# A fused decoder layer on one core: attention steps in another order, its rotation on VectorE, rotary tables in five parts, half of the first round's additions on VectorE

## The chip, the cores and the metric

The kernel runs on one core of one Trainium2 chip. The metric is device time in microseconds (us) from the start to the end of one execution; a few executions of the same kernel give the median and the interval that are shown below. Of one execution there is a profile: the time of every instruction on every engine. TensorE is called PE in it, VectorE DVE, ScalarE ACT, GpSimd POOL and SyncE SP.

## The reference, cut to what matters

One layer over 512 positions of 1024 features, in float32: a gated feed-forward block (FFN), a mixing block of three head groups side by side, and a second FFN. Each reads an RMS-normed copy of x and adds its result to x.

```python
x = x + 0.5 * swiglu(rms_norm(x, g_ffn1), w_gate1, w_up1, w_down1)
h = rms_norm(x, g_mix)
q, k, v, u, mq = split(h @ w_in)
q = rope_partial(rms_norm(q, g_q), positions)      # 16 of a head's 64 rows turn
k = rope_partial(rms_norm(k, g_k), positions)
y_attn = sliding_window_attention(q, k, v, sinks)  # 8 heads, 2 k/v heads, window 128
y_conv = silu(layer_norm(depthwise_conv(a * sigmoid(gate), 31 taps)))
y_mem  = memory_cross_attention(rms_norm(mq), mk, mv)   # 4 heads, 256 memory rows
x = x + concat(y_attn, y_conv, y_mem) @ w_out
x = x + 0.5 * swiglu(rms_norm(x, g_ffn2), w_gate2, w_up2, w_down2)
```

## The kernel before, in words

Activations stand transposed: features on the 128 partitions, the 512 positions along a row. A float32 product is made of three products of rounded halves: `whi` and `wlo` are the two halves of a weight tile, `xh`/`xl`, `yh`/`yl`, `hh`/`hl`, `bh`/`bl` those of activations. A 512-column product is the line trio L347, L348, L349 (`mm3`); a 256-column one is L444, L445, L446. Each weight tile comes by DMA into `wraw`; ACT rounds it (`whi`, L167) and DVE subtracts (`wlo`, L168). Four buffers each hold these halves, used in turn, so a cast waits until PE has read the tile of four turns before. A scheduler places the instructions of each engine in one fixed order; an instruction that waits holds up all that stands behind it on its engine.

**FFN.** 22 tiles f of hidden features. From the fifth on, `fast(f)` makes gate and up by seven 256-column block products instead of eight. Partial sums leave PSUM by ACT copies into `kept` (L455, L459, L461), DVE adds them (L464, L475, L479), ACT takes silu (L465) and rounds the hidden tile (`hh`, L402), DVE subtracts (`hl`, L403). `down(r, g)` multiplies finished tiles with the down weights, in rounds r of some tiles each, two outputs d per weight tile g in round 0. A result is added to x by DVE (L506), or in round 0 by an ACT copy (L502) and a POOL transfer that adds in memory (L503). `rotary` makes the sine and cosine tables for the later rotation: a range reduction on DVE (L701 to L713), then Sin, Abs, Sin on ACT (L714, L715, L717). It is one hook behind tile 9 of the first FFN.

**Mixing.** The steps stand in the list `ORDER`, written by hand: each name is a function that records its instructions for all engines. `pX` is the projection of tile X (48 instructions: L347 to L349), `sumX` the sums of squares of two tiles over a head, on PE with a 2-column operand (L814, from ACT's squares L805), `facX` their inverse roots, a chain of small operations on DVE (L826 to L834, L332 to L337), `ropeX` the rotation (L839 to L842), `scoresX` the score products on PE (L865; 64 rows, 128 or 256 columns), `softX` the masked maximum on DVE (L883, then `neg` L892, L895) and the exponentials on ACT (L901), `weightsX` the division (L914 to L923), `turnX` transposes of the weights on PE (L936) with copies to `pt` (L939), `valuesX` the products with v (L950) with `yh`/`yl` (L966, L967), `outD_KS` the output product of tile D over the parts KS of y, `c` one more tap of the convolution on DVE (L793, two instructions), `ln_...` its layer norm. S0 to S3 are the four pairs of query heads, M0 and M1 the memory heads, K the keys. The rotation is a shuffle on DVE (L839), a product with the sine table on POOL (L840), a product with the cosine table on DVE (L841), and an addition (L842). Behind the list come the output products over parts 4 and 5 (weights `wb`), then over 6 and 7 (`wc`), whose `yh`/`yl` are the convolution's and come from `ln_swish` (transposes L1026, a multiplication L1084, silu L1085, then L966, L967).

## Time and profile before

| | |
|---|---|
| median of 3 runs | 875.81 us (874.29 to 877.52) |
| the profiled execution's own time | 874.01 us |
| its span, first to last instruction | 872.2 us |
| PE busy | 863.5 us (99%) |
| DVE busy | 697.7 us (80%) |
| ACT busy | 449.2 us (51%) |
| POOL busy | 46.3 us (5%) |
| mean granted clock of TensorE | 0.996 |

The span lies 1.8 us below the execution's own time; that rest is start and end. A busy share is a mean over stages. The granted clock is a share of TensorE's upper level (2.4 GHz), so 0.50 is the lower one, 1.2 GHz.

### The profile page before, as it was taken

How to read it: one execution, taken by the hardware profiler on the slowest of the kernel's cores; microseconds unless marked ns; L12 is line 12 of the kernel's file. 1: busy time of each engine (PE TensorE's matmuls, PEld its weight loads, DVE VectorE, ACT ScalarE, POOL GpSimd, SP SyncE). 2: the span in 40 equal slices, each digit the busy share in tenths (PEclk: the TensorE clock that was granted, in tenths of full speed). 3: DMA queues.
4: the chain of work that ended last, by engine and by line, in shares of the span. 5: the costliest groups of instructions: out<-in, count | busy, mean ns of one | idle time of the engine just before them, and what ended most of it. 6: DMA issues, size and time to landing. Idle time of an engine off the chain costs nothing.

```text
span 872.2 us, 14898 instructions
## 1 busy us (share of the span) xinstructions
PE 863.5 (99%) x5929; PEld 775.5 (89%) x5929; DVE 697.7 (80%) x1150; ACT 449.2 (51%) x747; POOL 46.3 (5%) x44
## 2 busy tenths in 40 slices
PE   8999999999999999999999999999999999999998
PEld 5889999899999998888676788889999999999998
DVE  7997888987878786769998876997887878777772
ACT  7456554544654454433937864455554454545440
POOL 0011000000110000300010021011000000000000
PEclk9999999999999999999998999999999999999999
DMA  7327534233433334222010332337534333433312
GB/s 272 120 84 180 128 110 126 88 118 101 141 123 124 122 97 127 77 93 61 12 50 13 95 104 81 97 88 174 128 112 126 95 108 93 121 98 107 113 49 97
DMA packets 35526, 92.71 MB, mean 106 GB/s; under 512 B 3328, under 2 KB 5888, under 8 KB 35456
## 3 DMA queue, kind: packets, MB, share of 16 engines
q1 hardware_dynamic: 32000, 85.99, 31.6%
q0 software_dynamic: 2304, 4.20, 3.0%
q10 hardware_dynamic: 1152, 1.57, 0.6%
q8 instruction: 46, 0.75, 0.4%
q14 instruction: 24, 0.20, 0.1%
HBM read 85.45 MB, written 2.10 MB: 100 GB/s over the span
## 4 chain that ended last, share of the span: by engine, by line
PE 93%; DVE 4%; issue 1%; ACT 1%; DMA 1%; SPq 0%; ACTq 0%
PE mm L347 15%; PE mm L348 15%; PE mm L349 15%; PE mm L444 11%; PE mm L445 11%; PE mm L446 11%; PE sc L444 2%; PE sc L445 2%; PE sc L446 2%; PE tp L936 1%; PE sc L347 1%; PE sc L349 1%; PE sc L348 1%; PE tp L950 1%; PE sc L865 1%
## 5 line engine op out<-in xcount | busy, mean ns | idle before, releaser
L444 PE MATMUL mm<-bh,whi 128*128 128x256 f32 x864 | 239.3, 277 | 0.9 <-ACT kept L455 0.4
L445 PE MATMUL mm<-bl,whi 128*128 128x256 f32 x864 | 238.6, 276 | 0.0
L446 PE MATMUL mm<-bh,wlo 128*128 128x256 f32 x864 | 238.6, 276 | 0.0
L167 ACT CAST whi<-wraw 128x1024 fp32r<-128x1024 f32 (+2 forms) x122 | 124.2, 1021 | 106.9 <-PE mm L348 46.8
L168 DVE TENSOR_TENSOR wlo<-wraw,whi 128x1024 fp32r<-128x1024 f32 (+2 forms) x122 | 145.0, 1190 | 37.0 <-ACT whi L167 36.6
L444 PEld LDWEIGHTS mm<-bh,whi 128*128 128x128 f32 x864 | 162.3, 188 | 2.2 <-ACT kept L459 0.8
L445 PEld LDWEIGHTS mm<-bl,whi 128*128 128x128 f32 x864 | 162.2, 188 | 0.8
L446 PEld LDWEIGHTS mm<-bh,wlo 128*128 128x128 f32 x864 | 162.2, 188 | 0.0
L349 PE MATMUL mm<-hh,wlo 128*128 128x256 f32 (+1 forms) x496 | 161.3, 326 | 0.0
L348 PE MATMUL mm<-hl,whi 128*128 128x256 f32 (+1 forms) x496 | 161.2, 326 | 0.0
L347 PE MATMUL mm<-hh,whi 128*128 128x256 f32 (+1 forms) x496 | 160.6, 326 | 0.0
L168 DVE TENSOR_TENSOR wlo<-s,whi 128x1024 fp32r<-128x1024 f32 x72 | 87.9, 1222 | 34.5 <-ACT whi L167 34.5
L349 PEld LDWEIGHTS mm<-hh,wlo 128*128 128x128 f32 x496 | 93.2, 188 | 9.2
L347 PEld LDWEIGHTS mm<-hh,whi 128*128 128x128 f32 x496 | 93.2, 188 | 8.0
L348 PEld LDWEIGHTS mm<-hl,whi 128*128 128x128 f32 x496 | 93.2, 188 | 7.9
L167 ACT CAST whi<-s 128x1024 fp32r<-128x1024 f32 x72 | 75.5, 1050 | 45.1 <-PE mm L445 40.5
L347 PE MATMUL mm<-xh,whi 128*128 128x512 f32 x192 | 76.2, 401 | 0.8 <-ACT whi L179 0.8
L348 PE MATMUL mm<-xl,whi 128*128 128x512 f32 x192 | 75.7, 394 | 0.6 <-DVE xl L359 0.5
L349 PE MATMUL mm<-xh,wlo 128*128 128x512 f32 x192 | 75.9, 396 | 0.0
L465 ACT ACTIVATE t<-t 128x512 f32<-128x512 f32 x36 | 22.8, 632 | 61.5 <-DVE t L464 61.3
L167 ACT CAST vhi<-wraw 128x512 fp32r<-128x512 f32 x36 | 22.4, 621 | 58.2 <-PE sc L445 45.4
L506 DVE SCALAR_TENSOR_TENSOR x<-mm,x 128x512 f32<-128x512 f32 x72 | 48.6, 684 | 4.0 <-PE mm L349 3.9
(244 smaller groups left out, 1404.7 us busy)
## 6 DMA issues: line engine op xcount, KB each, us to landing
wraw<-in_wgu SPq DMA_DIRECT2D x86, 512.0 KB, 3.5
wraw<-in_wd SPq DMA_DIRECT2D x44, 512.0 KB, 3.6
wraw<-in_win SPq DMA_DIRECT2D x12, 512.0 KB, 3.4
x<-t POOLq DMA_DIRECT2D x16, 256.0 KB, 5.6
out<-t SPq DMA_DIRECT2D x7, 256.0 KB, 2.0
x<-in_xT SPq DMA_DIRECT2D x3, 512.0 KB, 6.8
wraw<-in_wout_a SPq DMA_DIRECT2D x6, 256.0 KB, 2.7
wraw<-in_wgu SPq DMA_DIRECT2D x4, 256.0 KB, 4.9
```

Of the source, the lines that this page charges most:

```text
L167: nc.scalar.copy(hi[:, :cols], raw[:, :cols])
L168: nc.vector.tensor_tensor(lo[:, :cols], raw[:, :cols], hi[:, :cols].bitcast(F32), op=ALU.subtract)
L347: PE.matmul(ps[:, t], wh[:, w], hi(k)[:, t], start=one, stop=False, skip_group_check=cut > 1)
L348: PE.matmul(ps[:, t], wh[:, w], lo(k)[:, t], start=False, stop=False, skip_group_check=cut > 1)
L349: PE.matmul(ps[:, t], wl[:, w], hi(k)[:, t], start=False, stop=end, skip_group_check=cut > 1)
L444: PE.matmul(ps, wh[:, c], bh[k][:, block], start=one, stop=False, skip_group_check=not first)
L445: PE.matmul(ps, wh[:, c], bl[k][:, block], start=False, stop=False, skip_group_check=not first)
L446: PE.matmul(ps, wl[:, c], bh[k][:, block], start=False, stop=end, skip_group_check=not first)
L465: ACT.activation(g, g, AF.Silu)
L506: DVE.scalar_tensor_tensor(o, ps, 0.5, xd, op0=ALU.mult, op1=ALU.add)
L865: PE.matmul(banks[h][:, i * ML + c.start : i * ML + c.stop], self.q[rows, n * P : (n + 1) * P], self.kt[rows, ks], start=True, stop=True, ...
L936: PE.transpose(ps[:, i * P : (i + 1) * P], self.p[n, h][:, c : c + P], ident)
```

## The change

Five edits. (1) `ORDER` is another list: `out0_01` stands ahead of `sumB` instead of behind `weightsS1`, `valuesM1` behind `ropeS1`, several `c` stand elsewhere, and `ln_swish` is out of the list and is called behind the third output product over parts 4 and 5. (2) The sine product of the rotation is on DVE. (3) `rotary` is five functions, hooked behind tiles 9 to 13, that work in the tables themselves instead of in work buffers; Abs comes ahead of the first Sin. (4) Round 0 adds with DVE for d = 4 to 7 (g of 2 and 3) and through ACT and POOL only for d = 0 to 3. (5) The two weight tiles `wmk` get an address offset of 128.

```diff
--- before.py
+++ after.py
@@ -65,11 +65,11 @@
 ORDER = """
 c c c c pM0 pM1 sumM c c facM pK c scoresM00 scoresM01 c softM01 softM00 weightsM0 c sumK c pV scoresM11
 scoresM10 turnM00 turnM01 softM10 c softM11 weightsM1 facK c valuesM0 normK turnV c ropeK c turnM10 turnM11
-pS0 ropeS0 pS1 sumA valuesM1 facA ropeS1 c c pS2 c scoresS01 c scoresS00 softS00 softS01 c weightsS0 ropeS2
-pS3 scoresS10 softS10 c scoresS11 sumB facB turnS00 turnS01 softS11 scoresS20 c weightsS1 c out0_01 c c c
-valuesS0 turnS10 scoresS21 out1_01 softS20 out1_2 ropeS3 softS21 c c turnS11 weightsS2 valuesS1 scoresS30
-turnS20 out0_2 scoresS31 softS31 turnS21 softS30 out2_0123 out1_3 weightsS3 c out0_3 valuesS2 out3_0123 c
-ln_mean ln_square turnS30 ln_var out4_0123 c turnS31 out5_0123 valuesS3 ln_swish
+pS0 ropeS0 pS1 sumA facA ropeS1 c valuesM1 pS2 scoresS01 scoresS00 softS00 softS01 c weightsS0 ropeS2 c
+pS3 scoresS10 softS10 scoresS11 out0_01 sumB facB c turnS00 turnS01 softS11 scoresS20 c weightsS1 c c
+valuesS0 turnS10 scoresS21 out1_01 softS20 out1_2 ropeS3 softS21 c c turnS11 weightsS2 c valuesS1 scoresS30
+turnS20 out0_2 scoresS31 softS31 turnS21 softS30 out2_0123 out1_3 weightsS3 c c out0_3 valuesS2 c c out3_0123 c
+c ln_mean ln_square turnS30 ln_var out4_0123 turnS31 out5_0123 valuesS3
 """.split()
 TILES = [s[1:] for s in ORDER if s[0] == "p"]
 
@@ -262,7 +262,7 @@
                 W.add(down(*d), 128)
             if memory and f == MEM_F:
                 for t in range(2):
-                    W.add(flat(a["wmk"][t]))
+                    W.add(flat(a["wmk"][t]), 128)
                 for c in range(2):
                     W.add(flat(a["wmv"][:, 4 * c : 4 * c + 4]))
         r = len(ROUNDS) - 1
@@ -497,7 +497,7 @@
                         True, True, woff=lo - j * (hi - lo), cut=1 + (last and r > 0 and not cut),
                     )
                     xd = x[:, d, t0:t1]
-                    if r == 0:
+                    if r == 0 and g < 2:
                         o = work()
                         ACT.activation(o, ps, AF.Copy, scale=0.5)
                         POOL.dma_start(xd, o, accum_op=ALU.add)
@@ -695,29 +695,39 @@
         q = 2.0 ** -21
         B2 = round(rest / q) * q
         B3 = rest - B2
-        posi = tmp.tile([P, T], I32, tag="t", name="posi", bufs=5)
-        nc.scalar.dma_start(posi, a["pos"])
-        ang, k1, u, k2 = work(), work(), work(), work()
-        DVE.tensor_copy(ang, posi)
-        DVE.tensor_scalar(ang, ang, par[:, C_INVF : C_INVF + 1], None, op0=ALU.mult)
-        DVE.tensor_scalar(k1, ang, 1.0 / (TWO_PI * 4096.0), MAGIC, op0=ALU.mult, op1=ALU.add)
-        DVE.tensor_scalar(k1, k1, MAGIC, 4096.0, op0=ALU.subtract, op1=ALU.mult)
-        for c in (A1, A2, A3):
-            DVE.scalar_tensor_tensor(ang, k1, -c, ang, op0=ALU.mult, op1=ALU.add)
-        DVE.scalar_tensor_tensor(u, k1, -A4, ang, op0=ALU.mult, op1=ALU.add)
-        DVE.tensor_scalar(k2, u, 1.0 / TWO_PI, MAGIC, op0=ALU.mult, op1=ALU.add)
-        DVE.tensor_scalar(k2, k2, MAGIC, None, op0=ALU.subtract)
-        for c in (B1, B2, B3):
-            DVE.scalar_tensor_tensor(ang, k2, -c, ang, op0=ALU.mult, op1=ALU.add)
-        DVE.scalar_tensor_tensor(ang, k1, -A4, ang, op0=ALU.mult, op1=ALU.add)
-        DVE.tensor_scalar(ang, ang, 3.1415925, -3.1415925, op0=ALU.min, op1=ALU.max)
-        ACT.activation(sinb, ang, AF.Sin)
-        ACT.activation(k1, ang, AF.Abs)
-        DVE.tensor_scalar(k1, k1, -1.0, math.pi / 2, op0=ALU.mult, op1=ALU.add)
-        ACT.activation(cosb, k1, AF.Sin)
+        ang, k1, st = sinb, cosb, {}
+
+        def reduce(t, k, parts):
+            for c in parts:
+                DVE.scalar_tensor_tensor(t, k, -c, t, op0=ALU.mult, op1=ALU.add)
+
+        def start():
+            posi = tmp.tile([P, T], I32, tag="t", name="posi", bufs=5)
+            nc.scalar.dma_start(posi, a["pos"])
+            DVE.tensor_copy(ang, posi)
+            DVE.tensor_scalar(ang, ang, par[:, C_INVF : C_INVF + 1], None, op0=ALU.mult)
+            DVE.tensor_scalar(k1, ang, 1.0 / (TWO_PI * 4096.0), MAGIC, op0=ALU.mult, op1=ALU.add)
+            DVE.tensor_scalar(k1, k1, MAGIC, 4096.0, op0=ALU.subtract, op1=ALU.mult)
+
+        def turns():
+            u, k2 = work(), work()
+            DVE.scalar_tensor_tensor(u, k1, -A4, ang, op0=ALU.mult, op1=ALU.add)
+            DVE.tensor_scalar(k2, u, 1.0 / TWO_PI, MAGIC, op0=ALU.mult, op1=ALU.add)
+            DVE.tensor_scalar(k2, k2, MAGIC, None, op0=ALU.subtract)
+            st["k2"] = k2
+
+        def end():
+            reduce(ang, k1, (A4,))
+            DVE.tensor_scalar(ang, ang, 3.1415925, -3.1415925, op0=ALU.min, op1=ALU.max)
+            ACT.activation(k1, ang, AF.Abs)
+            ACT.activation(sinb, ang, AF.Sin)
+            DVE.tensor_scalar(k1, k1, -1.0, math.pi / 2, op0=ALU.mult, op1=ALU.add)
+            ACT.activation(cosb, k1, AF.Sin)
+
+        return start, lambda: reduce(ang, k1, (A1, A2, A3)), turns, lambda: reduce(ang, st["k2"], (B1, B2, B3)), end
 
     load, piece, sums, p1, p2 = memory()
-    hooks = {9: [rotary]}
+    hooks = {9 + i: [part] for i, part in enumerate(rotary())}
     hooks[MEM_F - 3] = [lambda: load(0), lambda: load(1)]
     hooks[MEM_F - 2] = [lambda: piece(0), lambda: piece(1), lambda: load(2), lambda: load(3)]
     hooks[MEM_F - 1] = [lambda: piece(2), lambda: piece(3)]
@@ -837,7 +847,7 @@
         s = work()
         u = work()
         DVE.stream_shuffle(s, q, list(range(8, 16)) + list(range(0, 8)) + list(range(16, 32)))
-        POOL.tensor_tensor(s, s, sinb, op=ALU.mult)
+        DVE.tensor_tensor(s, s, sinb, op=ALU.mult)
         DVE.tensor_tensor(u, q, cosb, op=ALU.mult)
         DVE.tensor_tensor(q, u, s, op=ALU.add)
 
@@ -1092,7 +1102,7 @@
         "sumB": lambda: sums("B", "S2", "S3"), "facB": lambda: factors("B", "S2", "S3"),
         "sumK": lambda: sums("K", "K"), "facK": key_factor, "normK": key_norm, "turnV": value_turn,
         "ropeK": lambda: rope(kT), "c": lambda: pump(1),
-        "ln_mean": ln_mean, "ln_square": ln_square, "ln_var": ln_var, "ln_swish": ln_swish,
+        "ln_mean": ln_mean, "ln_square": ln_square, "ln_var": ln_var,
     }
     for t in TILES:
         steps["p" + t] = lambda t=t: project(t)
@@ -1119,6 +1129,8 @@
     wb = [W.next(), W.next()]
     for d in range(6):
         mm3(banks[d], *wb[d // 4], [4, 5], yhk, ylk, False, False, woff=4 - 2 * (d % 4))
+        if d == 2:
+            ln_swish()
     wc = [W.next(), W.next()]
     for d in range(6):
         mm3(banks[d], *wc[d // 4], [6, 7], yhk, ylk, False, True, woff=6 - 2 * (d % 4))
```

From line 700 on, numbers of the changed kernel are other ones; from L724 on they are 10 higher (L814 is L824, L865 is L875, L936 is L946, L966 is L976).

PE at the sums of S2 and S3 (`t` is a square, `sc` and `mm` hold scores, `tp` transposes), before:

```order
L865 MATMUL mm_4836<-kT,q_4625 128x256
L814 MATMUL tp_4841<-pair,t_4713 128x2 x4
L814 MATMUL tp_4841<-pair,t_4811 128x2 x4
L865 MATMUL sc_4915<-kT,q_4712 128x128
L865 MATMUL sc_4916<-kT,q_4712 128x128
L936 MATMUL tp_4876<-ident,p_4733 128x128
L865 MATMUL sc_4915<-kT,q_4712 128x256
L936 MATMUL tp_4876<-ident,p_4733 128x128 x2
L936 MATMUL tp_4876<-ident,p_4746 128x128
L936 MATMUL tp_4883<-ident,p_4746 128x128 x3
L865 MATMUL sc_4916<-kT,q_4712 128x256
L347 MATMUL mm_4944<-yh_3974,whi_4594 128x512
```

The same place in the changed kernel:

```order
L875 MATMUL mm_4820<-kT,q_4615 128x256
L347 MATMUL mm_4831<-yh_3964,whi_4584 128x512
L348 MATMUL mm_4831<-yl_3972,whi_4584 128x512
L349 MATMUL mm_4831<-yh_3964,wlo_4585 128x512
L347 MATMUL mm_4831<-yh_3965,whi_4584 128x512
L348 MATMUL mm_4831<-yl_3973,whi_4584 128x512
L349 MATMUL mm_4831<-yh_3965,wlo_4585 128x512
L824 MATMUL tp_4838<-pair,t_4701 128x2 x4
L824 MATMUL tp_4838<-pair,t_4797 128x2 x4
L946 MATMUL tp_4875<-ident,p_4717 128x128 x3
L946 MATMUL tp_4875<-ident,p_4730 128x128
L875 MATMUL sc_4914<-kT,q_4700 128x128
```

Six 512-column products now stand ahead of the sums; behind the sums come transposes and scores alone, up to the products of `valuesS0`.

DVE in tile 9 of the first FFN, where the rotary tables were made (`t_1568` and `t_1569` are the angle and its turns), before:

```order
L464 TENSOR_TENSOR t_1596<-mm_1592,kept_1594 128x512
L709 TENSOR_SCALAR t_1571<-t_1571 128x512
L506 SCALAR_TENSOR_TENSOR x<-mm_1691,x 128x512
L711 SCALAR_TENSOR_TENSOR t_1568<-t_1571,t_1568 128x512
L168 TENSOR_TENSOR vlo_1793<-wraw_1501,vhi_1792 128x512
L711 SCALAR_TENSOR_TENSOR t_1568<-t_1571,t_1568 128x512
L475 TENSOR_TENSOR t_1597<-kept_1595,mm_1591 128x512
L711 SCALAR_TENSOR_TENSOR t_1568<-t_1571,t_1568 128x512
L168 TENSOR_TENSOR wlo_1706<-s_29_1680,whi_1705 128x1024
L712 SCALAR_TENSOR_TENSOR t_1568<-t_1569,t_1568 128x512
L479 TENSOR_TENSOR t_1597<-t_1597,t_1596 128x512
```

The same tile in the changed kernel:

```order
L464 TENSOR_TENSOR t_1569<-mm_1565,kept_1567 128x512
L126 TENSOR_TENSOR s_32_1818<-wraw_1662 128x512
L129 TENSOR_TENSOR s_32_1819<-wraw_1636,wraw_1662 128x512
L506 SCALAR_TENSOR_TENSOR x<-mm_1664,x 128x512
L127 TENSOR_TENSOR s_32_1818<-wraw_1636,s_32_1818 128x512
L128 TENSOR_TENSOR s_32_1819<-wraw_1636,s_32_1818 128x512
L168 TENSOR_TENSOR vlo_1769<-wraw_1493,vhi_1768 128x512
L475 TENSOR_TENSOR t_1570<-kept_1568,mm_1564 128x512
L479 TENSOR_TENSOR t_1570<-t_1570,t_1569 128x512
L168 TENSOR_TENSOR wlo_1679<-s_29_1653,whi_1678 128x1024
```

L475 and L479, which together give the hidden tile, now stand next to each other here.

ACT at the end of the mixing block (`yh` of `conv` are parts 6 and 7; the 768-column casts belong to the last two output weights), before:

```order
L966 CAST yh_3979<-tp_5337 128x512
L1085 ACT_TABLE_LOAD
L1085 ACTIVATE conv<-conv,par 128x512 x2
L966 CAST yh_3980<-conv 128x512
L966 CAST yh_3981<-conv 128x512
L167 CAST whi_5373<-wraw_5290 128x768
```

In the changed kernel:

```order
L976 CAST yh_3969<-tp_5327 128x512
L1095 ACT_TABLE_LOAD
L1095 ACTIVATE conv<-conv,par 128x512 x2
L167 CAST whi_5350<-wraw_5280 128x768
L976 CAST yh_3970<-conv 128x512
L976 CAST yh_3971<-conv 128x512
```

The weight cast now stands ahead of the two casts of the convolution's result.

## Rows read from the trace of the kernel before

**Rows 1.** The page: busy us (share, instructions) and granted clock in 40 slices.

```profile
PE 863.5 (99%) x5929; PEld 775.5 (89%) x5929; DVE 697.7 (80%) x1150; ACT 449.2 (51%) x747; POOL 46.3 (5%) x44
...
PEclk9999999999999999999998999999999999999999
```

**Rows 2.** Waits of PE: line, releaser, total us, times, longest.

```profile
PE tp L814 <- ACT t L805: 1.8, 1, 1.8
...
PE tp L936 <- DVE yl L967: 0.4, 1, 0.4
PE mm L444 <- ACT kept L455: 0.4, 1, 0.4
PE mm L444 <- ACT kept L459: 0.3, 1, 0.3
```

**Rows 3.** Windows: length, busy us of each engine, granted clock, DMA share, GB/s.

```profile
430.88:456.35 25.47, 25.04 (x137) 18.23 (x135) 23.76 (x68) 10.10 (x24) 4.45 (x3) 1.00 0.17 52
456.35:459.17 2.82, 1.05 (x10) 0.96 (x8) 2.80 (x13) 2.82 (x11) 0.00 (x0) 1.00 0.00 0
...
461.66:468.48 6.82, 6.82 (x21) 4.15 (x21) 6.82 (x35) 3.49 (x11) 1.17 (x1) 0.50 0.14 38
...
60.00:100.00 40.00, 40.00 (x281) 36.81 (x280) 32.51 (x43) 23.18 (x36) 7.06 (x8) 1.00 0.61 145
```

**Rows 4.** Timeline of PE, mixing: start, duration, line, operation, [idle before, releaser].

```profile
430.65 0.39 PE L349 MATMUL mm<-xh,wlo 128*128 128x512 f32 x1
430.88 0.39 PE L347 MATMUL mm<-xh,whi 128*128 128x512 f32 x1
431.70 0.63 PE L936 MATMUL tp<-ident,p 128*128 128x128 f32 x4 [0.43 <-DVE yl L967]
...
464.54 0.63 PE L348 MATMUL mm<-yl,whi 128*128 128x512 f32 x1
464.96 0.63 PE L349 MATMUL mm<-yh,wlo 128*128 128x512 f32 x1
```

**Rows 5.** Timeline of DVE, two taps of the convolution.

```profile
436.26 1.78 DVE L793 SCALAR_TENSOR_TENSOR conv<-pad,par,conv 128x512 f32<-128x512 f32 x1
...
439.17 0.74 DVE L793 SCALAR_TENSOR_TENSOR conv<-pad,par,conv 128x512 f32<-128x512 f32 x1
```

**Rows 6.** Timeline of POOL, the rotation of S0.

```profile
436.00 1.49 POOL L840 TENSOR_TENSOR t<-t,sinb 128x512 f32<-128x512 f32 x1 [5.46 <-issue]
```

**Rows 7.** Timeline of ACT, the first exponential of S0 and the square of S3.

```profile
453.97 0.49 ACT L901 ACTIVATE p<-p,neg,qfac 128x128 f32<-128x128 f32 x1 [5.19 <-DVE neg L895]
...
458.55 0.57 ACT L805 ACTIVATE t<-mm 128x512 f32<-128x512 f32 x1
```

**Rows 8.** Timeline of PE in tile 9 of the first FFN.

```profile
163.47 0.28 PE L445 MATMUL mm<-bl,whi 128*128 128x256 f32 x1
163.59 0.28 PE L446 MATMUL mm<-bh,wlo 128*128 128x256 f32 x1
164.27 0.39 PE L444 MATMUL mm<-bh,whi 128*128 128x256 f32 x1 [0.41 <-ACT kept L455]
...
166.25 0.38 PE L444 MATMUL mm<-bh,whi 128*128 128x256 f32 x1 [0.34 <-ACT kept L459]
```

**Rows 9.** Timeline of ACT there.

```profile
163.87 0.35 ACT L455 COPY kept<-mm 128x256 f32<-128x256 f32 x1
```

**Rows 10.** Timeline of DVE at the end of mixing: the layer norm's multiplication.

```profile
505.82 1.28 DVE L1084 TENSOR_TENSOR conv<-conv,tp 128x512 f32<-128x512 f32 x2 [0.19 <-PE tp L1026]
```

**Rows 11.** Timeline of ACT at the end of mixing.

```profile
506.55 1.52 ACT L1085 ACTIVATE conv<-conv,par 128x512 f32<-128x512 f32 x2 [0.34 <-DVE conv L1084]
507.98 1.12 ACT L966 CAST yh<-conv 128x512 fp32r<-128x512 f32 x2
509.51 0.83 ACT L167 CAST whi<-wraw 128x768 fp32r<-128x768 f32 x1 [0.41 <-PE mm L348]
```

**Rows 12.** Timeline of ACT in an early tile of the second FFN.

```profile
608.44 0.38 ACT L459 ACTIVATE kept<-mm 128x256 f32<-128x256 f32 x1
```

## Prediction

> **What bounds the kernel now.** I read the page first, for the engine that is never idle: PE is busy in 99% of the span [rows 1], and DVE and ACT, at 80% and 51%, matter only where PE waits for them. So I read PE's waits next [rows 2]: one of 1.8 us for the squares of S3 (L805), three of 0.3 to 0.4, and some at the start of the program that no edit touches. The reader is to see how little that is: with these waits alone the change could be worth no more than 3 us. The third view is the granted clock. The page shows one slice of forty below full speed [rows 1], and the windows place it: from 461.66 to 468.48 the clock is 0.50, the level of 1.2 GHz, while PE is busy throughout [rows 3]. Just before, from 456.35 to 459.17, PE had worked 1.05 of 2.82 us [rows 3]; the rest, 1.77, is the long wait. So that wait costs twice, itself and the half clock behind it.
>
> Why did PE wait there? The square (L805) begins at 458.55, behind the exponentials of S0, which begin at 453.97 after ACT stood 5.19 us for DVE's `neg` [rows 7]. DVE is late because it is full: 23.76 of 25.47 us up to 456.35 [rows 3]. And part of its busy time is a stall: with POOL's sine product running (436.00, 1.49 us) a tap of the convolution takes 1.78 us, where another takes 0.74 [rows 5, 6]. That is 1.04 lost by each of the five rotations.
>
> **The change part by part.** The sum goes by the profiled execution, 874.01 us, which is 1.80 below the median of 875.81; I take the difference in us from the one to the other.
>
> *Sine product on DVE.* It adds five instructions of the kind of a 512-column operation with two inputs. Such a one starts 0.6 to 0.7 after the one before (0.74 for a tap [rows 5]); it takes away the stall of 1.04 and the wait for POOL's 1.49 inside each rotation. So DVE gains 0.3 to 0.4 per rotation, and three to four rotations stand ahead of S0's masks: 1 to 1.6. With the taps that `ORDER` puts elsewhere I work the masks out some 2.1 earlier, so the exponentials begin at about 451.9 instead of 453.97, and the square of S3 is done at about 457.05 instead of 459.1 [rows 7].
>
> *The small gap.* At 430.88 a product is followed by a transpose only 0.82 later, where 0.23 is the usual distance [rows 4]: 0.59 lost to a `yl` that stood behind a divided row slowed by POOL's product for the keys. In the new order nothing slow stands ahead of it. **Gain 0.6**, bounds 0 and 0.6.
>
> *The long wait.* `out0_01` ahead of `sumB` gives PE six products of 0.23 [rows 4], 1.4 us of work, and PE comes 0.6 earlier: it reaches the sums at about 456.35 - 0.6 + 1.6 = 457.35, the 1.6 with the two changes of operand shape. The square is ready at 457.05. **Gain 1.8**; the margin is 0.3 only, and if the masks come just 1 us earlier, about 0.8 of the wait stays. Bounds 0.8 and 1.8.
>
> *The half clock.* In the low stretch products stand 0.42 apart instead of 0.23 [rows 4], so 6.82 us of it are the work of 3.7: **gain 3.1** if the clock stays up, and 0 if it falls again for as long. Here a rule speaks against the change. The rows show a busy PE losing its clock after a stretch of waiting, of 2-column sums, transposes and 64-row scores; they do not show which of these did it. The Trainium skill says in "TensorE: Matmul & The Clock Gate", "Part 4: PE-mode transpose", that transposes don't count as a busy PE in the way that products do. By that the filler now stands on the wrong side: behind the sums there are only transposes and scores until `valuesS0`, some 8 us, where before the six products stood in their middle; the sum would have 0 in place of 3.1. No run so far tells the two apart, since in the rows the wait and the light work come together. I take 3.1, as the wait goes and as elsewhere in mixing such light work stands between projections at a clock of 1.00 [rows 3], and leave the other case much room.
>
> *`ln_swish` later.* The transposes L1026 now stand behind the third output product, with 18 products of 0.23 behind them until parts 6 and 7 are wanted: 4.1 us. The chain needs a multiplication of 0.64 (1.28 for two), 1.52 of silu, now the weight cast of 0.83, one `yh` of 0.56, and a `yl` of 0.64: 4.2, and some 0.1 to 0.2 at each hand-over [rows 10, 11]. Before, the weight cast stood behind (509.51) and waited for PE [rows 11], and the chain had over 2 us to spare. **Loss 0.6**, bounds 0 and 1.5. Behind this wait stand the last products over parts 6 and 7 only.
>
> *Rotary in five parts.* In tile 9 PE goes from 163.59 to 164.27, 0.68 where 0.12 is usual [rows 8]: 0.56 lost to the copy at 163.87 [rows 9], which stood behind a late hidden tile and behind Sin and Abs. The second wait, of 0.34 [rows 8], costs 0.5 in the same proportion. In the new order L475 and L479 of this tile are neighbours and ACT has no table work, so both go: **gain 1.1**. The same instructions come back in tiles 10 to 13, at most two of 0.6 between L475 and L479; those are hidden as long as ACT has idle time ahead of its copies. Bounds 0.5 and 1.1.
>
> *Round 0.* Per FFN four ACT copies and four POOL transfers go, and four DVE additions of about 0.7 come: 2.8 us, into 7.5 us that DVE is idle from 60 to 100 [rows 3]. That hides them in the sum, not always in place: the scheduler now puts a `wlo` between L475 and L479 of tile 5 in the first FFN and one sum of weights there in the second, so `hh` comes later and a weight cast goes ahead of it. The copy that PE needs next stands behind both; at 608.44 it is already just in time [rows 12]. **Loss 0.5** for both FFNs, bounds 0 and 1.2.
>
> *The offset of `wmk`.* 48 products; it moves nothing in time that PE waits for. Even 0.005 each, half a digit of the rows, is 0.2: **0.1**, bounds 0 and 0.2.
>
> Sum: 0.6 + 1.8 + 3.1 - 0.6 + 1.1 - 0.5 + 0.1 = 5.6 of gain, so 868.4 for the profiled execution and 870.2 for the median; I say 870.3.
>
> **The rivals.** A measurement here can tell about 0.5%, 4.4 us: faster means below 871.4, slower above 880.2.
>
> *The clock falls again* behind the moved products. For it: the page's rule above, and that the low stretch lies just where the work is light. Against it: the wait is gone. Gain 5.6 - 3.1 = 2.5, time 873.3.
>
> *Another wait takes the place of the long one.* The margin at the sums is 0.3, and the copies of the weights (L939) for `valuesS0` stand in ACT's queue behind the exponentials. A wait of 1 to 1.5 there, and 1.5 instead of 0.6 before parts 6 and 7, leave a gain of 3.2 to 3.7: 872.1 to 872.6, with the clock up.
>
> *The rotary and FFN edits do nothing*, since other work in tiles 12 and 13 makes L479 as late as before: 1.1 less, 871.4, on the line.
>
> *Slower.* The clock falls and stays low. Before, it came back at 468.48, after six products at 0.42 [rows 3, 4]; now those six are ahead and the next come in smaller groups between transposes. At 0.50 each us of low clock costs 0.45 (3.1 of 6.82), and without its 3.1 the change has 5.6 to give: from 12 us of low clock on the time is above 875.8, and a stretch of 22 us, from 460 to the end of the attention steps, gives 870.2 + 9.9 = 880.1. Against it: the one low stretch of before ended after 6.8 us, and nowhere else in mixing did the clock fall [rows 1, 3].
>
> **How the numbers follow.** I give the forecast 0.5 (868 to 871.8), the fallen clock 0.32, the other wait 0.13 with the idle edits in it, the long low clock 0.05. The low end takes all bounds on the gain's side (0.6 + 1.8 + 3.1 + 1.1 + 0.2 = 6.8, so 869.0) and 1.1 more for a median of a few runs, which spans 1.5 to either side; the high end takes the fallen clock with 1.1 of the losses' bounds: 867.9 to 874.4. Faster by 0.5% is nine tenths of the forecast and some of the other wait: 0.50; within 0.5% the fallen clock and the rest: 0.45; slower: 0.05.
>
> **What would show it.** In the profile after: no gap at the first transposes of M1's weights; POOL without L850; taps all near 0.74; S0's exponentials before 452.5 less the gain so far; no wait of PE at L824 for L815, or one under 0.3; a granted clock of 1.00 in every slice, or else a low stretch behind the moved products, which decides most of the rest; a wait before the products over parts 6 and 7 of 0.3 to 1; no wait for L455 in tile 9; and waits of 0.2 to 0.6 in tile 5 of the FFNs. A low stretch of 3 us or more makes the forecast wrong, and so does a PE wait over 1 us at the sums.

## The result and the profile after

The changed kernel takes 867.55 us (median of 6 runs, 866.59 to 869.57), the kernel before 875.25 beside it (6 runs, 874.02 to 877.52). The ratio is 0.9908, 95% interval 0.9894 to 0.9922: faster by 7.7 us in the medians. The forecast was a gain of 5.6, to 870.3, with a range from 867.9: the direction is right, and the time lies 0.35 below the range. Two executions of the kernel before that took 1067 and 4919 us are left out of everything below. The two profiled executions differ by 6.3 (874.01 and 867.69), their spans by 6.3 (872.2 and 865.9).

The page of the changed kernel, busy time and granted clock, answers to [rows 1]:

```profile
PE 858.4 (99%) x5929; PEld 773.6 (89%) x5929; DVE 701.9 (81%) x1163; ACT 446.5 (52%) x739; POOL 32.3 (4%) x31
...
PEclk9999999999999999999999999999999999999999
```

The same 5929 instructions of PE take 5.1 us less busy time, so most of the gain stands in no list of waits. All waits of PE that the trace of the changed kernel lists (line, releaser, total us, times, longest), to be held against [rows 2]:

```profile
PE tp L302 <- DVE pair L315: 1.2, 1, 1.2
PE mm L347 <- DVE s L893: 1.0, 1, 1.0
PE mm L347 <- ACT whi L179: 0.9, 1, 0.9
PE mm L348 <- DVE xl L359: 0.5, 1, 0.5
PE mm L347 <- ACT yh L976: 0.3, 1, 0.3
```

The four waits of [rows 2] are gone. L302, L179 and L359 belong to the start of the program. Two waits are new: 1.0 for the masks (L893), which the forecast did not have, and 0.3 for `yh`, which it had. Windows of the changed kernel in mixing (length, busy us of PE, PEld, DVE, ACT, POOL, clock, DMA share, GB/s), against [rows 3]:

```profile
448.00:455.09 7.09, 7.09 (x40) 5.43 (x39) 7.09 (x36) 5.35 (x19) 0.20 (x1) 1.00 0.08 34
455.09:458.00 2.91, 2.91 (x25) 2.62 (x24) 2.73 (x14) 2.91 (x9) 0.00 (x0) 1.00 0.00 0
458.00:461.50 3.50, 3.50 (x17) 2.38 (x16) 2.96 (x26) 3.03 (x10) 0.00 (x0) 0.51 0.30 75
```

PE is busy in every microsecond of these 13.5, and still the clock drops to its 1.2 GHz level at 458, for 3.4 us instead of 6.8. That is only one execution: of the six timed ones three have a mean clock of 1.000, the others 0.997 to 0.999. (A 0.999 need not be a loss in mixing: in two later profiles with that mean the low clock lies in the last 0.8 and 1.4 us, where PE has no work left.) The timeline of PE (start, duration, operation, idle before) shows where the filler stands, and the two new waits:

```profile
454.86 0.40 PE L349 MATMUL mm<-yh,wlo 128*128 128x512 f32 x1
455.09 1.84 PE L824 MATMUL tp<-pair,t 128*128 128x2 f32 x16
...
473.69 0.50 PE L347 MATMUL mm<-yh,whi 128*128 128x512 f32 x1 [0.97 <-DVE s L893]
...
505.96 0.73 PE L347 MATMUL mm<-yh,whi 128*128 128x512 f32 x2 [0.34 <-ACT yh L976]
```

The sums follow the last product at once. The timeline of ACT shows why, against [rows 7]:

```profile
449.74 0.50 ACT L911 ACTIVATE p<-p,neg,qfac 128x128 f32<-128x128 f32 x1 [3.72 <-DVE neg L905]
...
454.32 0.58 ACT L815 ACTIVATE t<-mm 128x512 f32<-128x512 f32 x1
```

The square is done at 454.90, PE arrives at 455.09: a margin of 0.2, where the forecast had 0.3. The changed kernel is 2.1 ahead when mixing begins; with that added, the exponentials, the end of the square and PE's arrival come at 451.9, 457.0 and 457.2 on the time of before, and the forecast had 451.9, 457.05 and 457.35.

Taking the PE instructions of both traces in their order, the lead of the changed kernel grows in few places: 0.2 at the start, 0.2 in tile 5 of the first FFN, 1.3 in tile 9, 0.4 from 273 to 287, 4.1 in mixing, 0.4 in tile 5 of the second FFN. That is 6.6, of which the end of the program gives 0.3 back. The 0.4 behind 273 is not at the products with `wmk`, which take 5.62 us in both traces: it is at the 48 products with `wmv` and the block products after them, whose distance falls from 0.118 to 0.113.

### The profile page after: what moved, and what is told of

It reads as the page before. It is cut to its first block, busy times and chain, and to the rows that moved or that the text cites. A ratio compares the mean times of both kernels' runs of the same rounds, so it can differ in the third digit from the quotient of the medians.

```text
span 865.9 us, 14855 instructions
## 1 busy us (share of the span) xinstructions
PE 858.4 (99%) x5929; PEld 773.6 (89%) x5929; DVE 701.9 (81%) x1163; ACT 446.5 (52%) x739; POOL 32.3 (4%) x31
## 4 chain that ended last, share of the span: by engine, by line
PE 98%; DVE 1%; DMA 1%; issue 0%; ACT 0%; SPq 0%; DVEq 0%
PE mm L347 16%; PE mm L349 16%; PE mm L348 16%; PE mm L444 11%; PE mm L446 11%; PE mm L445 11%; PE sc L444 2%; PE sc L446 2%; PE sc L445 2%; PE tp L946 1%; PE sc L347 1%; PE sc L349 1%; PE sc L348 1%; PE sc L875 1%; PE mm L875 1%; PE tp L960 1%
## 5 line engine op out<-in xcount | busy, mean ns | idle before, releaser
L506 DVE SCALAR_TENSOR_TENSOR x<-mm,x 128x512 f32<-128x512 f32 x80 | 54.0, 684 | 4.0 <-PE mm L349 3.9
```

Of the source, the lines that this page charges most:

```text
L506: DVE.scalar_tensor_tensor(o, ps, 0.5, xd, op0=ALU.mult, op1=ALU.add)
```

## The experiments

Two readings of the missing 2 us stood against each other. **Clock theory**: the one profile of before shows a short loss of clock, and the median execution loses more, so the mixing edits give more in the median than in the pair of profiles. **Sizes theory**: the terms of the FFN edits were mis-sized, and the surplus is there. All comparisons were timed in 5 rounds beside the kernel before; "changed kernel" means all five edits.

| kernel | median | ratio to before, 95% interval | mean clock of its executions |
|---|---|---|---|
| before, again | 874.18 | 0.9989 (0.9979 to 0.9998) | 0.9952 |
| mixing edits alone | 869.10 | 0.9936 (0.9918 to 0.9954) | 0.9997 |
| other edits alone | 873.07 | 0.9977 (0.9967 to 0.9988) | 0.9947 |
| changed, old list | 869.84 | 0.9935 (0.9919 to 0.9950) | 0.9967 |
| changed, sine product on POOL | 869.57 | 0.9941 (0.9925 to 0.9958) | 0.9963 |
| changed, out0_01 back | 871.37 | 0.9959 (0.9945 to 0.9974) | 0.9966 |
| changed, out0_01 in two halves | 867.77 | 0.9914 (0.9894 to 0.9933) | 0.9997 |
| changed, out0_2 later | 867.45 | 0.9912 (0.9897 to 0.9928) | 0.9994 |
| changed, ln_swish earlier (same order) | 868.38 | 0.9919 (0.9901 to 0.9938) | 0.9985 |
| changed, rotary in one piece | 868.76 | 0.9932 (0.9914 to 0.9949) | 0.9987 |
| changed, round 0 all by transfers | 868.17 | 0.9931 (0.9906 to 0.9955) | 0.9997 |
| changed, round 0 all on DVE | 868.22 | 0.9914 (0.9894 to 0.9934) | 0.9993 |
| round 0 edit alone | 874.68 | 0.9984 (0.9970 to 0.9999) | 0.9947 |
| rotary edit alone | 874.70 | 0.9989 (0.9979 to 1.0000) | 0.9945 |

**The kernel before, again.** No edit.

> The kernel before, unchanged, for what its executions share. Clock theory: the 2.65 us by which the median missed the forecast are mostly that the profiled execution of before (874.0) was one of its shortest; executions of before differ by the length of the half-clock stretch behind the wait for the squares, so this profile or the clocks of the runs show more lost clock where the time is longer, 1 us of time for each 0.002 of mean clock. Rival (sizes theory): the low stretch is 6 to 7 us again, and the clocks of the runs do not go with their times.

This profiled execution takes 876.12, and its low stretch is longer, 10.2 us instead of 6.8 (window of PE's low clock, columns as above):

```profile
459.37:469.61 10.24, 9.68 (x31) 6.55 (x31) 9.04 (x55) 6.88 (x20) 0.27 (x1) 0.50 0.07 22
```

Of 81 executions of before that were timed in these comparisons, 29 have a mean clock of 0.996 (median 874.28) and 51 of 0.994 (875.92), one 0.995. So a mean clock lower by 0.002 goes with 1.64 us, and half of the 3.4 us by which the two low stretches differ is 1.7: the same loss. The profile on which the forecast stands is of the rarer, shorter kind. The same execution holds something else, that the clock theory does not explain. The timelines of DVE and PE in tile 5 of the first FFN:

```profile
78.38 0.69 DVE L126 TENSOR_TENSOR s<-wraw 128x512 f32<-128x512 f32 x1 [2.87 <-DMA wraw<-in_wgu]
```

```profile
86.54 0.38 PE L444 MATMUL mm<-bh,whi 128*128 128x256 f32 x1 [0.96 <-ACT kept L459]
```

DVE waits 2.87 for a weight load, all that follows it is late, and PE loses 1.3 there against the changed kernel, where the first profile lost 0.2. So each theory has hold of a part. And the ratio of 0.9989 for an unchanged kernel says what such a comparison can't tell: effects of 0.1%, 1 us, even where the interval leaves out 1.

**The two halves of the change.** The mixing edits alone, and the others alone:

```diff
-ORDER = (the list before), ln_swish in it
+ORDER = (the new list), ln_swish behind the third output product
-        POOL.tensor_tensor(s, s, sinb, op=ALU.mult)
+        DVE.tensor_tensor(s, s, sinb, op=ALU.mult)
```

```diff
-    hooks = {9: [rotary]}
+    hooks = {9 + i: [part] for i, part in enumerate(rotary())}
-                    if r == 0:
+                    if r == 0 and g < 2:
-                    W.add(flat(a["wmk"][t]))
+                    W.add(flat(a["wmk"][t]), 128)
```

> The edits to mixing alone (the list of steps, ln_swish, the sine product on DVE); FFNs, rotary and wmk as before. Clock theory: the median falls by 5.5 to 6 us, more than the 4.3 by which PE leads at the end of mixing in the two profiles. Sizes theory: 4.3, and the surplus lies in the other edits. Forecast: 4.9.

> The other edits alone (rotary in five parts, half of round 0 on DVE, the offset of wmk); mixing as before. Forecast: 0.7 gained. Sizes theory, by PE's lead in the profile after: 2.0 (1.2 rotary, 0.2 wmk, 0.1 and 0.3 in tile 5 of the FFNs, the rest at the start); if it also holds the part of the median that no lead shows, 3.4. Clock theory: 1.7 to 2.0. The low stretch in mixing stays 6 to 7 us by all.

The mixing edits give 5.6 by the ratio (4.0 to 7.2), the others 2.0 (1.1 to 2.9); together 7.6, against 7.7 for the whole in the medians. The forecast's 4.9 lies inside the first interval, its 0.7 below the second; the larger miss, 1.3, is outside mixing, and little more than the 1.0 at which the unchanged kernel came out. Five of the six executions with the mixing edits have a clock of 1.000, the profiled one too, and there PE needs 5.1 us less for mixing than in the first profile of before and 6.3 less than in the second. In the profile of the other edits the low stretch is 10.2 us (457.04 to 467.28), not the 6 to 7 expected: again an execution of the longer kind.

**Sine product or list?** Each undone in the changed kernel; with the old list `ln_swish` is back in it.

```diff
-ORDER = (the new list), ln_swish behind the third output product
+ORDER = (the list before), ln_swish in it
```

```diff
-        DVE.tensor_tensor(s, s, sinb, op=ALU.mult)
+        POOL.tensor_tensor(s, s, sinb, op=ALU.mult)
```

> The changed kernel with the old list of steps and the old place of ln_swish; the sine product stays on DVE. If the stall of DVE by POOL's product made the masks late, the wait for the squares of S3 shrinks from 1.8 to 0.3 or less and the gap behind 430 goes; then the clock may stay up, and the time is within 1.5 us of the changed kernel. If the place of out0_01 is what fills the wait, the wait stays over 1 us, the low stretch stays near 6 us, and the time is 3 to 4.5 us above the changed kernel.

> The changed kernel with the rotation's sine product back on POOL; the new list of steps stays. Stall theory (the port time that POOL takes from DVE makes the masks of S0 late): taps of 1.7 to 1.8 us come back, S0's exponentials begin 1.5 to 2.5 us later, PE waits 0.5 to 1.5 for the squares of S3 although out0_01 stands ahead, and the time is 2 to 4 above the changed kernel. Order theory (the new list alone is enough): under 1 us above it, no wait over 0.5 at the sums.

With the old list the wait for the square shrinks to 0.4 and the exponentials begin at 450.22: the sine product on DVE alone takes most of the wait away. Its time, 2.3 above the changed kernel, lies between the two forecasts: in its profile the wait for the masks (1.0) is gone, but one of 1.6 for a `yl` (L977) is new, and its six clocks are 0.995 to 0.998. With the sine product on POOL the stalled tap is back (timeline of DVE):

```profile
433.97 1.78 DVE L803 SCALAR_TENSOR_TENSOR conv<-pad,par,conv 128x512 f32<-128x512 f32 x1
436.87 0.74 DVE L803 SCALAR_TENSOR_TENSOR conv<-pad,par,conv 128x512 f32<-128x512 f32 x1
```

and PE waits 0.9, not at the sums but at the transposes behind them, and from the middle of that wait on the clock is low for 10.2 us (windows of that kernel):

```profile
458.00:459.18 1.18, 0.89 (x7) 0.48 (x6) 1.18 (x9) 0.89 (x3) 0.00 (x0) 1.00 0.00 0
459.18:469.42 10.24, 9.64 (x50) 7.10 (x51) 8.07 (x46) 7.02 (x23) 1.70 (x1) 0.50 0.10 27
```

That is one execution: its clock is 0.994, and three of the six have 0.998. By the ratios each alone, with the other edits, gives 5.2 to 5.7, and both 8.0. The other edits are 2.0 of that, so either takes 3 to 4 of mixing's gain and the second adds 2 to 3: both work on the same wait. The stall theory holds in its mechanism: the tap is back, the exponentials begin 1.3 later (1.5 to 2.5 expected), PE waits, and the time is 2.0 above the changed kernel. The gap at the first transposes of M1's weights is back too (0.41), and with the old list and the sine product on DVE it is not there: that gap is the sine product's. The order theory, that the list alone is enough, falls.

**What costs the clock: the wait or the light work?** First `out0_01` back behind the weights of S1, so that PE comes to the sums earlier and only light work follows; then its six products in two halves.

```diff
 out0_01 back:
-scoresS11 out0_01 sumB facB c turnS00 turnS01 softS11 scoresS20 c weightsS1 c c
+scoresS11 sumB facB c turnS00 turnS01 softS11 scoresS20 c weightsS1 out0_01 c c
 in two halves:
-scoresS11 out0_01 sumB facB c turnS00 turnS01 softS11
+scoresS11 out0_0 sumB facB c turnS00 out0_1 turnS01 softS11
```

> The changed kernel with out0_01 back behind the weights of S1; all else as changed. PE then comes to the sums 1.4 earlier than in the changed kernel (453.7) while the square of S3 ends at 454.9: a wait of 1.0 to 1.3. If a wait of PE is what costs the clock, a low stretch of 6 us or more follows and the time is 3 to 4 above the changed kernel. If the light work costs it (2-column sums, transposes, 64-row scores), the wait costs itself alone, the low stretch is 3 to 4 us as in the profile of the changed kernel, and the time is 1 to 1.5 above.

> The changed kernel with the six moved products cut in two: three ahead of the sums, three among the transposes behind them. Light-work theory: the low stretch of 3.4 us at 458 goes in all executions (clock 1.000 in each), against a wait of 0.3 to 0.7 at the sums; the median is 0 to 0.7 below the changed kernel. If a wait costs the clock, the wait at the sums brings a low stretch and the median is 0.5 to 2 above.

With `out0_01` back the wait at the sums is only 0.3, and the low stretch in its profile is short, 3.4 us (windows of that kernel):

```profile
457.00:461.81 4.81, 4.52 (x35) 3.66 (x32) 4.81 (x27) 4.40 (x15) 0.20 (x1) 1.00 0.00 0
461.81:465.23 3.42, 3.42 (x15) 2.44 (x14) 2.54 (x22) 2.91 (x10) 0.00 (x0) 0.50 0.00 0
```

as the light-work theory had it. Yet the median is 3.8 above the changed kernel, more than the 1 to 1.5 expected, and the nine executions have clocks of 0.994 to 0.998, on the mean 0.0024 below the changed kernel: by 1.64 us for 0.002 that is 2.0 of the 3.8. So other executions lose more clock than the profiled one, no trace shows behind what, and this run does not decide between the two theories.

The profiled execution, the slowest of the nine, has its time from elsewhere. Mixing is 2.2 longer in it than in the changed kernel's profile at the same 3.4 us of low clock (new waits of 0.5 before the transposes L1082 and 0.8 for copies of weights, none for the masks), and the first FFN, which the edit does not touch, is 5.1 longer. There the block products stand 0.118 apart, at a clock of 1.00 and without a wait (timeline of PE, ten distances in that kernel, then in the changed one):

```profile
99.72 0.28 PE L445 MATMUL mm<-bl,whi 128*128 128x256 f32 x1
...
100.90 0.28 PE L446 MATMUL mm<-bh,wlo 128*128 128x256 f32 x1
```

```profile
99.83 0.28 PE L446 MATMUL mm<-bh,wlo 128*128 128x256 f32 x1
...
100.96 0.28 PE L444 MATMUL mm<-bh,whi 128*128 128x256 f32 x1
```

With the halves the clock does not fall although PE waits 0.94 in the midst of that place (timeline of PE):

```profile
457.37 0.48 PE L347 MATMUL mm<-yh,whi 128*128 128x512 f32 x1
457.68 0.40 PE L348 MATMUL mm<-yl,whi 128*128 128x512 f32 x1
...
460.87 0.33 PE L946 MATMUL tp<-ident,p 128*128 128x128 f32 x1 [0.94 <-ACT pt L949]
```

Four of its six executions have 1.000, two 0.999, and in the profiled one, a 0.999, the low clock lies behind PE's last product (864.85 to 865.7). Of twelve executions of the changed kernel's program (six of them under the name `ln_swish` earlier, below) seven have 0.999 or more, so six of six point to the halves and do not prove them. The time is the same as that of the changed kernel: what the clock gives, the new wait for the copies takes.

A wait alone can cost the clock too. In the profile of the round 0 edit alone, further on, PE waits 1.87 among 256-column products of the first FFN, with none of the light work near, and this follows (window of that kernel):

```profile
167.51:170.92 3.41, 3.41 (x18) 3.41 (x17) 3.41 (x6) 2.60 (x5) 0.00 (x0) 0.50 0.56 156
```

So the clock fell on light work without a wait (the changed kernel), and behind a wait without light work. With both together it stayed low longest: of the eleven profiles in which it fell in mixing, the six with a wait of 0.9 to 1.8 at the sums or the transposes behind them have 6.8 us once and 10.2 five times, the five with a wait of 0.4 or none 3.4 each. Yet it does not fall every time: the repeated profile of the changed kernel's program (`ln_swish` earlier, below) has 1.00 all through mixing.

**The new wait for the masks, and that for `yh`.**

```diff
-turnS20 out0_2 scoresS31 softS31 turnS21
+turnS20 scoresS31 softS31 out0_2 turnS21
```

```diff
-        if d == 2:
+        if d == 1:
             ln_swish()
```

> The changed kernel with out0_2 behind scoresS31 instead of ahead of it: three products of 0.23 go between the last scores of S3 and out2, which waits 1.0 for the masks of those scores to free a PSUM bank. If that bank is the cause, the wait falls by 0.5 to 0.7 and the time by as much; if another wait follows (the copies to pt), the time does not change.

> The changed kernel with ln_swish called behind the second instead of the third output product over parts 4 and 5. Six more products of 0.23 lie between its transposes and the first product over part 6, so the wait there (0.5 with the late start) goes: 0.3 to 0.5 faster, if the multiplication on DVE is not itself late. Rival: the layer norm's chain on DVE ends only then, PE waits at the transposes instead, no change.

With `out0_2` later, the wait for the masks is gone, and all waits of PE in mixing are these:

```profile
PE tp L946 <- ACT pt L949: 0.4, 1, 0.4
PE tp L960 <- ACT pt L949: 0.3, 1, 0.3
PE mm L347 <- ACT yh L976: 0.3, 1, 0.3
```

So what holds up `out2` is what the masks release, and three products fill that time. That it is the PSUM bank is argued from the releaser, the mask operation that reads the scores out of it; no run gave `out2` another bank. Mixing is only 0.2 shorter than in the profiles of the changed kernel's list that also keep the clock: the wait for copies in the second of these rows (0.5 from start to start) and longer distances elsewhere take 0.9 of the 1.1 back, and the median is unchanged (0.9912). Calling `ln_swish` one output product earlier tests nothing: in the trace PE and DVE have the same instructions in the same places as in the changed kernel, the transposes L1036 too, so neither reading was tried. It is the changed kernel timed once more, 868.38 with a ratio of 0.9919 against 867.55 and 0.9908, and says how far two measurements of one program lie apart: 0.8 us. Its wait for `yh` is again 0.34.

**Round 0 and rotary.** The changed kernel with each undone, with round 0 wholly on DVE, and each edit alone on before.

```diff
-                    if r == 0 and g < 2:
+                    if r == 0:            # all by transfers
+                    if r == 0 and g < 0:  # all on DVE
-    hooks = {9 + i: [part] for i, part in enumerate(rotary())}
+    hooks = {9: [rotary]}
```

> The changed kernel with all of round 0 added through ACT and POOL's transfers again. Transfer theory: the four adding transfers in each FFN delay a weight load, so DVE waits 1 to 3 us for a load ahead of tile 5 in some executions, PE waits 0.2 to 1.2 for a copy there, and the median is 1 to 1.5 above the changed kernel. By the forecast's term (DVE's additions cost 0.5) it is 0.5 below; by PE's lead of the two profiles alone 0.3 to 0.5 above.

> The changed kernel with all of round 0 added by DVE, no adding transfer left. Transfer theory (the transfers delay weight loads): another 0.3 to 1 faster, with a shorter wait of DVE for loads. Rival (DVE is the limit there: four more additions of 0.7 in each FFN, idle 4.3 of 40 us now): a wait for a copy in tile 5 of 0.3 to 1 comes back and the time is 0.5 to 1.5 above.

> The changed kernel with the rotary tables made in one piece in tile 9. Forecast's term: 1.1 above the changed kernel, by two waits of PE for copies in tile 9. By the profile of the mixing edits alone, where these two waits cost 2.2, it is 1.5 to 2.2 above.

> The kernel before with the round 0 edit alone. Transfer theory: with four adding transfers less in each FFN DVE waits 1.2 or less for a load ahead of tile 5 (1.7 and 2.9 in two profiles of before), PE's waits for a copy in tile 5 go (0 to 1.1 in the first FFN, 0.3 to 0.5 in the second), and the median falls by 0.6 to 1.3. Forecast's term: it rises by 0.5.

> The kernel before with the rotary edit alone. Forecast's term: 1.1 gained. If rotary holds the surplus, 1.7 to 2.4, as in the profile of the mixing edits alone, where the two waits in tile 9 cost 2.2; the waits in tile 5 stay.

DVE's wait for the weight load ahead of tile 5 goes with the number of adding transfers in the FFN. With eight it is 1.7 to 2.9 in all five profiles (before twice, mixing edits alone, rotary edit alone, all by transfers), with four 1.1 to 1.3 in all ten, here the round 0 edit alone:

```profile
77.06 0.69 DVE L126 TENSOR_TENSOR s<-wraw 128x512 f32<-128x512 f32 x1 [1.19 <-DMA wraw<-in_wgu]
```

The load itself shows it. With eight transfers it takes 4.5 to 5.7 us from issue to landing, with four 3.3 to 3.5. The issues (tile, queue, size, us to landing) in the first profile of before from 72 to 77 us, where one of the adding transfers runs beside the load, then in the changed kernel from 73 to 77:

```profile
wraw<-in_wgu SPq DMA_DIRECT2D x1, 512.0 KB, 4.5
x<-t POOLq DMA_DIRECT2D x1, 256.0 KB, 6.1
```

```profile
wraw<-in_wgu SPq DMA_DIRECT2D x1, 512.0 KB, 3.4
```

PE loses something in tile 5 in every profile with eight (0.1 to 1.3 in the first FFN, 0.3 to 1.6 in the second) and nothing in the other eleven. With no transfer left the load takes 3.8, and DVE does not wait, but for another reason: with its additions it comes to that place 3.0 later (79.59 instead of 76.58), when the load has just landed. So the step from four to none shows nothing more of the transfers; PE loses nothing in tile 5, and the time is that of the changed kernel, neither the 0.3 to 1 faster nor the 0.5 to 1.5 slower expected. Undoing the edit (all by transfers) costs 0.6 in the medians and 2.0 by the ratios, with intervals that overlap; the edit alone is worth 1.4 (0.1 to 2.6). These times hardly rise above the 1.0 of the unchanged kernel; the traces show the sign of the forecast's term to be wrong.

Rotary alone is worth 1.0 (0 to 1.8), and undoing it in the changed kernel costs 1.2 in the medians and 2.1 by the ratios (0.9932 against 0.9908), with intervals that overlap; in its profile the two waits in tile 9 cost 1.1 again. In the profile of the round 0 edit alone the copy in tile 9 that the forecast put at 0.56 costs 2.0:

```profile
167.06 0.38 PE L444 MATMUL mm<-bh,whi 128*128 128x256 f32 x1 [1.87 <-ACT kept L455]
```

So that loss too varies from one execution to the next, 0.25 to 2.0 for the first of its two waits, and here the 3.4 us of low clock shown above come behind it, 1.7 more. Below 1 us these medians don't tell the edits apart.

## Why the prediction was right and where it was wrong

*What bounds the kernel.* Right: PE, and the wait for the square with the low clock behind it is where the change acts.

*Sine product, small gap, long wait.* Right. Without POOL's product the taps take 0.74 to 0.75, the gap at 430.88 is gone, and the wait at the sums is gone with 0.2 to spare. From the first of the sums to the next product L814 takes 2.1 less. The steps of the chain came within 0.2 of the forecast, and the two single undoings bear out its cause. One reading in it was wide: not each of the five rotations lost 1.04 to a tap. In the trace of before four of the five stall one DVE operation by 1.0 to 1.2: the tap, a divided row (L921, 1.40 instead of 0.35) and two of 16 columns (L337, 1.27, and L1007, 1.38, instead of 0.17); beside the product at 441.63 none is stalled.

*The half clock, a gain of 3.1.* The direction was right, the size was off both ways. In the profile of the changed kernel the clock falls once more, for 3.4 us instead of 6.8: 1.7 came of the 3.1, and by the prediction's own sign (a low stretch of 3 us or more) the forecast was wrong there. In the medians the loss before was larger than the 6.8 us that I read: 51 of 81 executions are at 0.994, 1.6 us longer than those like the profiled one. From the mean clocks, 0.9947 to 0.999, the gain is 3.5; from the commonest executions, 0.994 to 1.000, it is 4.9. The step that failed is the sum's base, "I take the difference in us from the one to the other": a gain read from one execution, of the shorter kind, was set against a median of executions that lose more. The medians gained 1.4 more than the pair of profiles (7.7 against 6.3). The rival of the falling clock came half true. For it the prediction had the rule of the Trainium skill ("TensorE: Matmul & The Clock Gate", "Part 4: PE-mode transpose") that transposes don't count as a busy PE as products do. The trace agrees in part: a PE that was wholly busy with sums, transposes and 64-row scores had 0.51 from 458.00 to 461.50, but which of the three did it is not shown, and the same program kept 1.00 there in its other profile.

*`ln_swish` later, a loss of 0.6.* Right: 0.50 from start to start at 505.23, by the weight cast that moved ahead.

*Rotary, a gain of 1.1.* Right in the pair of traces (1.3); in four other profiles of the old form the two waits cost 1.0 to 2.4.

*Round 0, a loss of 0.5.* Wrong, in sign. The forecast counted the transfers as gone and gave them no price, since PE never waited for them by name. The step that failed is "2.8 us, into 7.5 us that DVE is idle": I asked what DVE gets to do, not what the eight transfers held up. In its place the runs show that the load lands sooner, DVE waits 0.5 to 1.7 less for it, and L475 begins 1.3 earlier (80.72 instead of 82.01). So the `wlo` that the forecast feared between L475 and L479 is there and does no harm: L479 still begins 0.3 earlier (82.46 instead of 82.80), and PE loses nothing in tile 5, where the pair's profile of before lost 0.2 in the first FFN and 0.4 in the second. The term was a gain of 0.6 in the pair, up to 2.1 in single profiles.

*The offset of `wmk`, a gain of 0.1.* Not shown. Its products take 5.62 us in both traces, and the gain of 0.4 behind them cannot be laid to it: in the repeated profile of the same program 0.118 stands at the products with `wmv` again and 0.113 at those with `wmk`.

*What was not in the sum.* The wait for the masks, 1.0 (1.1 from start to start). It hides that the rest of mixing gained more than forecast; in profiles that keep the clock mixing is 5.1 shorter in spite of it, against a forecast of 4.9.

Put together: the forecast was 5.6, the pair of profiles gives 6.3, the medians 7.7. That the pair comes so near the forecast is in part luck. Its mixing gained 0.8 less than forecast (4.1 instead of 4.9: 1.4 of the clock and 1.1 of the masks' wait are missing, and other places gave more), round 0 gave 1.1 more, and rotary and places outside the sum gave the rest. The other 1.4 lie in the sum's base, 1.2 of them in before, whose profile (874.01) is shorter than its median (875.25); its clock, 0.996 against a mean of 0.9947, goes with 1.1. Tenths mean nothing here: a comparison of before with itself came out at 0.9989, and the changed kernel in another comparison at 0.9919.

What makes executions at a clock of 1.000 differ by up to 5 us (866.14 to 871.57 with round 0 on DVE) is not shown for those executions. One thing that can do it is in the traces: 256-column products 0.118 apart instead of 0.113, which cost some 0.3 to 1.0 us in the first FFN of fifteen profiles and over 5 in that with `out0_01` back. Why they do is open.

## What to carry to other kernels

Before a gain is worked out from a trace, ask of each loss in it whether the next execution has it too: a second profile of the same kernel would have shown the longer low stretch and the late load. A transfer that no engine waits for by name can still hold up the loads that one does wait for; price it by the waits of the loads issued beside it. And where two edits work on one wait, either alone may give most of it, and the next wait, here for the masks and for copies, take a part back. Before a profile is used to explain a median, see that its time and its clock lie near the median's: that of `out0_01` back was the slowest of nine, for a reason that had nothing to do with the edit.

## What the runs showed of the hardware

The granted clock fell to 0.50 with PE busy throughout, on 2-column sums, transposes and 64-row scores, in some executions of a program and not in others: three of the six executions of the changed kernel have 1.000. It also fell behind a wait of 1.87 among 256-column products. The low stretches in the midst of the programs measured 3.4 us behind a wait of 0.4 or none and behind that of 1.87, and 6.8 or 10.2 where light work and a wait of 0.9 to 1.8 came together. Behind a wait of 0.94, with three 512-column products among the light work, the clock stayed up in the one profile taken.

A 512 KB weight load beside the transfers that add in memory took 4.5 to 5.7 us, and 3.3 to 3.5 where half of the transfers were gone. With a product of 1.3 to 1.7 us on POOL beside it an operation on DVE lost 1.0 to 1.2 in four of five rotations, whatever its size: a tap took 1.78 us instead of 0.74, one of 16 columns 1.27 instead of 0.17. Products of 256 columns stood 0.113 apart at a clock of 1.00, and 0.118 in stretches of every profile, without a wait that shows.
